# A hybrid-layer kernel: block-sum transfers issued one at a time at a fixed interval, unit loads written where a raw tile is freed, and a bank of its own for a unit's last product

## The chip, the cores and the metric

One core of a Trainium2 chip runs the whole program. The metric is the device time of one execution in microseconds (us), compared by medians of several runs. "Before" is the kernel that is changed, "after" the changed one.

## The reference

The layer has 512 tokens of width 1024. A normalised input is multiplied by one wide matrix `w_in`. Its columns feed a gated delta rule (branch a, 8 heads), a retention (branch b, 4 heads) and two gates. Both branches are projected, gated, mixed by `w_out` and added to the input; then a squared-ReLU MLP with 4096 hidden columns follows.

```python
xn = rmsnorm(x, n_mix_pre)
proj = xn @ w_in
qa, ka, va, za, beta_logit, a_dt, qb, kb, vb, gb, gate_a, gate_b = _split_cols(proj, IN_SIZES)
...
oa = chunk_gated_delta_rule(qa, ka, va, beta, g)
oa = rmsnorm(oa, norm_a) * jax.nn.silu(za.reshape(b, s, A_HEADS, A_DV))
ya = oa.reshape(b, s, A_V) @ w_br_a
...
ob = chunk_retention(qb, kb, vb)
ob = rmsnorm(ob, norm_b.reshape(B_HEADS, B_DV)) * jax.nn.silu(gb.reshape(b, s, B_HEADS, B_DV))
yb = ob.reshape(b, s, B_V) @ w_br_b
mix = (jax.nn.sigmoid(gate_a) * ya + jax.nn.sigmoid(gate_b) * yb) @ w_out
x = x + rmsnorm(mix, n_mix_post)
hn = rmsnorm(x, n_mlp_pre)
ff = jnp.square(jax.nn.relu(hn @ w_up)) @ w_down
return x + rmsnorm(ff, n_mlp_post)
```

## The kernel before

**Products.** Every fp32 operand is split into a high and a low part of type float32r, and a product is three matmuls (high by high, high by low, low by high). Weights come in tiles of 128 x 1024 floats (512 KB): SyncE (SP) issues the load into a tile `raw`, ScalarE (ACT) makes `whi` of it (line 145), VectorE (DVE) makes `wlo` (line 146), TensorE (PE) uses both. The raw tiles are a ring of two, from the first gate unit on of four (a second pool alternates); `whi` and `wlo` are rings of three. So a load waits for the split two or four loads earlier.

**Seven products for eight.** Ten large products are done by a scheme with seven block products instead of eight. It needs sums of weight blocks, and these are made in device memory by transfers alone: a copy job (line 166, on SP's queue) writes a block to a tile `sums`, and an add job (line 132, on GpSimd's queue, POOL, a transfer that accumulates) adds a second block to it. Each job moves 512 KB. There are 56 copies and 56 adds, for the late gates of branch a (`z`, 8 and 8), gate a (4 and 4), four value-and-gate units (4 and 4 each), gate b (4 and 4) and three groups of `w_down` (8 and 8 each), in that order. Adds of a set come after all copies of that set; from then on adds and copies of the next sets alternate.

**When a job is issued.** `pace` (line 112) is called behind each weight load. It compares `spent`, a planner's clock of PE's time, with `queued`, the time until which it takes the transfers to be busy, and issues jobs behind this load as long as `queued` is less than 6 us ahead. Each load counts 2.0 us, a copy 2.0 and an add 3.4, and nothing is issued until the clock is at 150. Several jobs can go behind one load. `issue_after` fixes where they stand in the order; a job runs when its engine's queue reaches it and its data are there.

**The order of each engine's work.** In the first phase (branch a, up to about 480 us of the trace) PE's order is planned by the same clock: steps of the delta rule (the chain) stand between pieces of large products (the fillers). Elsewhere, and on the other engines, a scheduler places instructions by priority; each engine then runs its list strictly in order.

**The units.** After the first phase, gate a, four value-and-gate units and gate b run through `seven` (line 243). In a unit the products are called 11, s3, s2, 12, 22, s1 and s4, each with two weight tiles (`ks` 0 and 1). Between them `plus` (line 249) adds one raw tile to another on DVE, so that a block sum that is not in memory is made from tiles that are there. s1 and s4 share a bank: `out(1, 1, c, u3, ...)` reads s1 from it, s4 is then accumulated on top, and `out(0, 1, c, p1, ...)` reads both. The six units are followed by the mix: PE multiplies `og` by the kept weights of `w_br_b`, transposes gated rows (`tr<-cmat,tb`), and multiplies by `w_out` (row tiles 2 and 3 together, then 0, then 1).

**Around the mix.** `acc` is read last in the gating (lines 1645 to 1649); then POOL loads the rows of x into it for the residual (line 1727), and the rows `post` and `wmlp` of the norm weights (line 1665). Line 1718 (`fw`) multiplies the product of `w_out` by `post`, which also frees the PSUM bank that the next row tile's product writes.

Of the kernel before, what the change touches and what calls it, by code (L numbers as in the profile page):

```python
# [15 lines left out]
ALU = mybir.AluOpType  # L16
# [9 lines left out]
OFF_BA = 6144  # L26
OFF_QB, OFF_KB, OFF_VB, OFF_GB = 6160, 7184, 8208, 10256
OFF_GA, OFF_GBR = 12304, 13328
JOBS_FROM, LOAD_US, COPY_US, ADD_US, BACKLOG = 150.0, 2.0, 2.0, 3.4, 6.0
SMALL_US, CONV_US, TOK_US, PK_US, INV_US, DB_US = 10.5, 6.5, 2.5, 2.0, 46, 1.2  # L30
VT_US, KS_US, PX_US, PC_US, GATE_US, FEAT_US, INV_PRIO, CONV_PRIO, SMALL_PRIO, KEY_PRIO, DECAY_US, AHEAD, TR_US, REC_PRIO, OUT_PRIO, SUM_PRIO = 2.5, 2.4, 3.5, 2.4, 11.0, 1.0, 0, 600, 800, 600, 20.0, 700, 2.2, 900, 900, 300
DFF = 4096
# [30 lines left out]
def hybrid_block_kernel(ctx: ExitStack, tc: tile.TileContext, a: dict, out: bass.AP):  # L63
    nc = tc.nc
# [9 lines left out]
    trickle, later_adds = [], []  # L74
    added, spent, queued, clocks = [False], [None], [JOBS_FROM], []
# [4 lines left out]
    psm = ctx.enter_context(tc.tile_pool(name="psm", bufs=4, space=PSUM))  # L80
# [15 lines left out]
    def weights(src, k0, nk, c0, ncols, keep=None, paced=True):  # L96

        n = nk * ncols
        i = next(loads)
        pool, tag = raw_pools[i % len(raw_pools)]  # L100
        raw = pool.tile([P, 1024], F32, tag=tag, name="raw", bufs=2)
        load = nc.sync.dma_start(
            raw[:, :n].rearrange("p (k c) -> p k c", k=nk),
            src[k0 * P : (k0 + nk) * P, c0 : c0 + ncols].rearrange("(k p) c -> p k c", p=P),
        )
        pace(load)
        with ExitStack() as behind:
            for mark in marks if i < 9 else ():
                behind.enter_context(tc.issue_after(mark.ins))
            return split_weights(raw, n, nk, keep, ahead[0] if i >= 6 else 0)  # L110

    def pace(load):

        if clocks:
            spent[0] = clocks[0].now
        if spent[0] is None:
            return
        queued[0] = max(queued[0], spent[0]) + LOAD_US
        with tc.issue_after(load.ins):
            while (trickle or later_adds) and queued[0] < spent[0] + BACKLOG:  # L120
                ready = bool(later_adds) and not any(job[0] is later_adds[0][2] for job in trickle)
                if ready and (added[0] or not trickle):
                    add_block()
                    queued[0] += ADD_US
                elif trickle:
                    copy_block()
                    queued[0] += COPY_US
                added[0] = not added[0]

    def add_block():  # L130
        dst, src, _ = later_adds.pop(0)
        tc.keep_in_program_order(nc.gpsimd.dma_start(dst, src, accum_op=ALU.add))  # L132

    def copy_block():
        sums, part, k = trickle.pop(0)
        sums.copy(part, k)

    def split_weights(raw, n, nk, keep=None, ahead=200):
        if keep is None:
            hi = ring.tile([P, 1024], F32R, tag="whi", name="whi")  # L140
            lo = ring.tile([P, 1024], F32R, tag="wlo", name="wlo")
        else:
            hi, lo = keep
        with tc.high_priority(ahead):
            nc.scalar.copy(hi[:, :n], raw[:, :n])  # L145
            nc.vector.tensor_tensor(lo[:, :n], raw[:, :n], hi[:, :n], ALU.subtract)  # L146
        return (
            hi[:, :n].rearrange("p (k c) -> p k c", k=nk),
            lo[:, :n].rearrange("p (k c) -> p k c", k=nk),
        )  # L150
# [74 lines left out]
    def bank(pool):  # L225
        if pool is psx:
            return [psx.tile([P, T], F32, tag="dl", name="dl", bufs=3) for _ in range(2)]
        return [psm.tile([P, T], F32, tag="mm", name="mm") for _ in range(2)]
# [13 lines left out]

    def seven(src, c1, c2, sums, product, temp, out):

        def times(pss, x, raws, first):
            for ks in range(2):
                product(pss, x, ks, split_weights(raws[ks], 1024, 2), first)

        def plus(dst, raws):
            with tc.high_priority(SUM_PRIO):  # L250
                for d, r in zip(dst, raws):
                    nc.vector.tensor_tensor(d, r, d, ALU.add)

        def raws(load, i):
            return [load(i, ks) for ks in range(2)]

        p1, u3 = [temp("p1") for _ in range(2)], [temp("u3") for _ in range(2)]
        x, y = raws(sums.first_raw, 1), raws(sums.raw, 3)
        a = bank(psx)
        times(a, "11", x, True)  # L260
        with tc.high_priority(400):
            for t in range(2):
                nc.scalar.copy(p1[t], a[t])
        b = bank(psm)
        times(b, "s3", y, True)
        plus(y, x)
        with tc.high_priority(400):
            for t in range(2):
                nc.vector.tensor_tensor(u3[t], p1[t], b[t], ALU.add)
        x = raws(sums.first_raw, 3)  # L270
        c = bank(psm)
        times(c, "s2", y, True)
        with tc.high_priority(400):
            for t in range(2):
                nc.vector.tensor_tensor(p1[t], p1[t], c[t], ALU.add)
                nc.vector.tensor_tensor(u3[t], u3[t], c[t], ALU.add)
        times(a, "12", x, False)
        out(0, 0, a)
        plus(x, y)
        d = bank(psm)  # L280
        times(d, "22", x, True)
        out(1, 0, d, u3, ALU.add)
        c = bank(psm)
        times(c, "s1", raws(sums.raw, 1), True)
        out(1, 1, c, u3, ALU.subtract)
        times(c, "s4", raws(sums.first_raw, 2), False)
        out(0, 1, c, p1, ALU.subtract)

    def token_product(quarters):

# [22 lines left out]
    def feature_major(src, xs, c0, ncols, kts, krow0=0):  # L313

        nf = ncols // P
        pss = [psm.tile([P, xs[0].shape[2]], F32, tag="mm", name="mm") for _ in range(nf)]
        step = 1024 // ncols
        for k0 in range(0, kts, step):
            wh, wl = weights(src, krow0 + k0, step, c0, ncols)
            for f in range(nf):  # L320
                fs = slice(f * P, (f + 1) * P)
                for kk in range(step):
                    kt = k0 + kk
                    mm3(
                        pss[f],
                        (wh[:, kk, fs], wl[:, kk, fs]),
                        (xs[0][:, kt, :], xs[1][:, kt, :]),
                        kt == 0,
                        kt == kts - 1,
                    )  # L330
        return pss
# [116 lines left out]
    with tc.tile_pool(name="xp", bufs=2) as xp:  # L448
# [3 lines left out]
        first = xp.tile([1, 1], F32, name="first", bufs=1)  # L452
# [15 lines left out]
        xts, raws = [], []  # L468
# [41 lines left out]
        def banks(n):  # L510
            return [psx.tile([P, 2, 256], F32, tag="dl", name="tr", bufs=3) for _ in range(n)]
# [32 lines left out]
        pss = banks(3) + [psx.tile([P, 2, 256], F32, tag="tr", name="tr", bufs=1)]  # L544
# [39 lines left out]
        pss = banks(3)  # L584
# [329 lines left out]
    def acc_rows(t, half):  # L914
        return acc_t[:, t, half * 512 : half * 512 + 512]
# [532 lines left out]
    with tc.tile_pool(name="pb", bufs=1) as pb_:  # L1448
# [11 lines left out]
        def values_and_gates(sums, c1, c2, g, out1, out2):  # L1460

            def out(th, ch, ps, u=None, op=None):
                for t in range(2):
                    row = 2 * th + t
                    if ch:
                        nc.vector.tensor_tensor(g[:, row, :], ps[t], u[t], op)
                        out2(row)
                    elif u is None:
                        out1(row, ps[t])
                    else:  # L1470
                        v = tmp("v_s")
                        nc.vector.tensor_tensor(v, ps[t], u[t], op)
                        out1(row, v)

            seven(w_in, c1, c2, sums, token_product(quarters), tmp, out)
# [90 lines left out]
        def gate_unit(sums, off, gated):  # L1566

            def out(th, ch, ps, u=None, op=None):
                for t in range(2):
                    src = ps[t]  # L1570
                    if u is not None:
                        src = tmp("g_s") if th and not ch else u[t]
                        with tc.high_priority(400):
                            nc.vector.tensor_tensor(src, ps[t], u[t], op)  # L1574
                    gated(2 * th + t, ch, src)

            seven(w_in, off, off + 512, sums, token_product(quarters), tmp, out)

        rows = None
        for h in range(4):  # L1580
# [13 lines left out]
            else:  # L1594
                for half, pss in branch_partial(w_br[1], og, 4 * (h - 1)):
                    for t in range(4):
                        dst = acc_rows(t, half)
# [32 lines left out]
        for pair in (1, 0):  # L1630
            pss = [[psm.tile([P, T], F32, tag="mm", name="mm") for _ in range(2)] for _ in range(2)]
            for i in range(2):
                t = 2 * pair + i
# [26 lines left out]
    with tc.tile_pool(name="pm", bufs=1) as pm:  # L1660
# [215 lines left out]
        for grp in range(4):  # L1876
            sq = Squares(grp)
            for half in range(2):
                for th in (None,) if grp or half else (1, 0):
                    tt = slice(0, T) if th is None else slice(256 * th, 256 * th + 256)  # L1880
                    pss = feature_major(w_up, [h[:, :, tt] for h in hn], grp * 1024 + half * 512, 512, 8)
# [57 lines left out]
```

## Time and profile before

| | |
|---|---|
| three runs | 1342.81, 1347.69 (median), 1348.85 us |
| profiled execution | 1347.26 us, of which the profile's span is 1345.5 us |
| PE, DVE, ACT, POOL busy | 98%, 69%, 47%, 6% of the span |
| clock granted to PE | full speed in all slices |
| transfers | 210.57 MB, a mean of 157 GB/s |
| copy jobs | 56 on SP's queue, median time to landing 7.4 us (`w_in`) and 12.5 us (`w_down`) |
| add jobs | 56 on POOL's queue, median 8.1 us (`w_in`), 14.3 us (`w_down`), 8.3 us (from `sums`) |
| weight loads | median 4.8 us (`w_in`), 4.0 us (from `sums`) |

PE is the engine to look at, so the useful views are its waits and the stretches in which its busy time falls short of the stretch's length. An idle engine elsewhere matters only where PE waits for it. Lines of the kind "start, duration, engine, line, operation" are from the timeline; in brackets stands the idle time before, and what ended it. `raw<-in_w_in_dram SPq` names a transfer by what it writes and reads and by the queue that issues it; its last number is the time from issue to landing.

### The profile page before, as it was taken

What the parts mean: (1) busy time and instruction counts of PE and PEld (TensorE: products, weight loads), DVE (VectorE), ACT (ScalarE), POOL (GpSimd) and SP (SyncE); (2) the same over time, 40 slices, a digit from 0 to 9 for tenths busy, and PEclk for the clock granted to TensorE, in tenths of its full rate; (3) what the DMA queues carried; (4) which work ended last, traced back from release to release, by engine and by line L of the source; (5) the groups of instructions that cost most, each with busy time, mean ns of one, the idle gap of its engine ahead of it and who ended that gap; (6) DMA issues with size and microseconds to landing.
All of it is one profiled execution on the core that took longest, in us unless ns stands there. A gap on an engine that the chain in (4) does not pass through costs nothing.

```text
span 1345.5 us, 17468 instructions
## 1 busy us (share of the span) xinstructions
PE 1324.8 (98%) x6615; PEld 1096.7 (82%) x6615; DVE 930.4 (69%) x1563; ACT 638.3 (47%) x1126; POOL 78.3 (6%) x83
## 2 busy tenths in 40 slices
PE   9999999999999999999999999999999999999997
PEld 7888888878788878888888888877889888888886
DVE  6889867486557567877577776878684745828535
ACT  5783436545534433543443343445255746346441
POOL 2100002010111100001001010000000000000000
PEclk9999999999999999999999999999999999999999
DMA  6322258777889764799398394445614443635421
GB/s 193 128 79 80 69 141 177 160 175 189 226 193 212 176 170 120 238 248 240 91 266 207 103 252 104 129 135 172 221 63 148 163 143 110 188 98 177 133 79 63
DMA packets 105701, 210.57 MB, mean 157 GB/s; under 512 B 6598, under 2 KB 30320, under 8 KB 105104
## 3 DMA queue, kind: packets, MB, share of 16 engines
q1 hardware_dynamic: 88592, 167.27, 39.7%
q0 software_dynamic: 14704, 35.30, 15.6%
q10 hardware_dynamic: 2320, 6.89, 1.4%
q8 instruction: 52, 0.85, 0.3%
q14 instruction: 33, 0.27, 0.1%
HBM read 205.21 MB, written 62.93 MB: 199 GB/s over the span
## 4 chain that ended last, share of the span: by engine, by line
PE 83%; DVE 7%; ACT 4%; DMA 4%; issue 1%; DVEq 0%; ACTq 0%
PE mm L654 15%; PE mm L303 14%; PE mm L93 11%; PE mm L92 11%; PE mm L94 11%; PE dl L303 9%; PE dl L654 5%; DVE wlo L146 2%; DMA raw<-in_w_in_dram 2%; DMA raw<-sums 2%; PE dl L94 1%; PE dl L92 1%; PE dl L93 1%; PE tr L383 1%; PE tr L663 1%
## 5 line engine op out<-in xcount | busy, mean ns | idle before, releaser
L145 ACT CAST whi<-raw 128x1024 fp32r<-128x1024 f32 x259 | 272.1, 1052 | 415.3 <-PE mm L93 104.1
L146 DVE TENSOR_TENSOR wlo<-raw,whi 128x1024 fp32r<-128x1024 f32 x259 | 316.0, 1223 | 216.3 <-ACT whi L145 215.1
L654 PE MATMUL mm<-actT,whi 128*128 128x512 f32 x448 | 144.3, 403 | 0.0
L303 PE MATMUL mm<-whi,xsum 128*128 128x512 f32 x384 | 122.0, 391 | 0.4 <-DVE u L1574 0.4
L94 PE MATMUL mm<-hn,wlo 128*128 128x512 f32 (+1 forms) x288 | 105.4, 366 | 0.0
L93 PE MATMUL mm<-hn,whi 128*128 128x512 f32 (+1 forms) x288 | 105.3, 366 | 0.0
L92 PE MATMUL mm<-hn,whi 128*128 128x512 f32 (+1 forms) x288 | 105.3, 366 | 0.0
L654 PEld LDWEIGHTS mm<-actT,whi 128*128 128x128 f32 x448 | 80.5, 188 | 14.9
L654 PE MATMUL mm<-actT,wlo 128*128 128x512 f32 x224 | 87.7, 392 | 0.0
L303 PEld LDWEIGHTS mm<-whi,xsum 128*128 128x128 f32 x384 | 72.0, 188 | 17.0 <-issue 2.2
L303 PE MATMUL mm<-wlo,xsum 128*128 128x512 f32 x192 | 75.1, 391 | 0.4 <-DVE wlo L146 0.4
L654 PE MATMUL mm<-whi,og 128*128 128x512 f32 x192 | 62.4, 397 | 0.0
L654 PE MATMUL mm<-whi,actT 128*128 128x512 f32 x176 | 61.3, 410 | 1.0 <-DVE qf L892 1.0
L94 PEld LDWEIGHTS mm<-hn,wlo 128*128 128x128 f32 x288 | 54.3, 189 | 8.8
L93 PEld LDWEIGHTS mm<-hn,whi 128*128 128x128 f32 x288 | 54.3, 189 | 8.7
L92 PEld LDWEIGHTS mm<-hn,whi 128*128 128x128 f32 x288 | 54.3, 189 | 8.7
L303 PE MATMUL dl<-whi,ffq 128*128 128x512 f32 x192 | 61.1, 389 | 0.0
L303 PE MATMUL dl<-whi,actT 128*128 128x512 f32 x192 | 61.1, 389 | 0.0
L1771 DVE TENSOR_TENSOR ffq<-r,ffq 128x512 fp32r<-128x512 f32 (+2 forms) x51 | 33.8, 678 | 29.1 <-ACT ffq L1771 29.0
L92 PE MATMUL mm<-actT,whi 128*128 128x512 f32 x128 | 51.5, 403 | 0.0
L132 POOL DMA_DIRECT2D sums<-in_w_in_dram x28 | 32.6, 1167 | 321.3 <-DMA sums<-in_w_in_dram 321.0
L94 PE MATMUL mm<-actT,wlo 128*128 128x512 f32 x128 | 50.8, 397 | 0.0
(393 smaller groups left out, 2881.8 us busy)
## 6 DMA issues: line engine op xcount, KB each, us to landing
raw<-in_w_in_dram SPq DMA_DIRECT2D x95, 512.0 KB, 4.8
raw<-sums SPq DMA_DIRECT2D x56, 512.0 KB, 4.0
raw<-in_w_up_dram SPq DMA_DIRECT2D x36, 512.0 KB, 3.9
sums<-in_w_in_dram SPq DMA_DIRECT2D x32, 512.0 KB, 7.4
sums<-in_w_in_dram POOLq DMA_DIRECT2D x28, 512.0 KB, 8.1
raw<-in_w_down_dram SPq DMA_DIRECT2D x26, 512.0 KB, 3.8
sums<-in_w_down_dram SPq DMA_DIRECT2D x24, 512.0 KB, 12.5
sums<-sums POOLq DMA_DIRECT2D x16, 512.0 KB, 8.3
```

The lines of the kernel that those rows point to most:

```text
L92: nc.tensor.matmul(ps, lh, rh, start=first, stop=False)
L93: nc.tensor.matmul(ps, lh, rl, start=False, stop=False)
L94: nc.tensor.matmul(ps, ll, rh, start=False, stop=last)
L132: tc.keep_in_program_order(nc.gpsimd.dma_start(dst, src, accum_op=ALU.add))
L145: nc.scalar.copy(hi[:, :n], raw[:, :n])
L146: nc.vector.tensor_tensor(lo[:, :n], raw[:, :n], hi[:, :n], ALU.subtract)
L303: m = nc.tensor.matmul(pss[t], lhs[i // 2], rhs[i % 2], start=first and k + i == 0, stop=k + i == 5, skip_group_check=not first,)
L383: nc.tensor.transpose(ps, src, ident)
L654: m = tc.keep_in_program_order(nc.tensor.matmul(*args, **kwargs))
L663: tc.keep_in_program_order(nc.tensor.transpose(ps, src, ident if by is None else by))
L1771: return nc.scalar.copy(dst[0], r), nc.vector.tensor_tensor(dst[1], r, dst[0], ALU.subtract)
```

## The change

Three edits. Jobs go one at a time: `pace` issues at most one job behind a load, and only when the planner's clock has reached `queued`, which then moves on by 8 us; it starts at 65 instead of 150. In `seven` the load of a following raw tile is written directly behind the product that uses the tile it takes the place of, one tile at a time, together with the `plus` for that tile. And s4 gets a bank of its own: the new DVE subtraction `p1 = c - p1` reads s1, and the last `out` adds s4's bank to it.

```diff
-JOBS_FROM, LOAD_US, COPY_US, ADD_US, BACKLOG = 150.0, 2.0, 2.0, 3.4, 6.0
+JOBS_FROM, JOB_US = 65.0, 8.0
...
-        queued[0] = max(queued[0], spent[0]) + LOAD_US
+        if spent[0] < queued[0] or not (trickle or later_adds):
+            return
+        queued[0] += JOB_US
         with tc.issue_after(load.ins):
-            while (trickle or later_adds) and queued[0] < spent[0] + BACKLOG:
-                ready = bool(later_adds) and not any(job[0] is later_adds[0][2] for job in trickle)
-                if ready and (added[0] or not trickle):
-                    add_block()
-                    queued[0] += ADD_US
-                elif trickle:
-                    copy_block()
-                    queued[0] += COPY_US
-                added[0] = not added[0]
+            ready = bool(later_adds) and not any(job[0] is later_adds[0][2] for job in trickle)
+            if ready and (added[0] or not trickle):
+                add_block()
+                added[0] = False
+            else:
+                copy_block()
+                added[0] = True
...
-        def times(pss, x, raws, first):
+        def times(pss, x, raws, first, then=lambda ks: None):
+            out = []
             for ks in range(2):
                 product(pss, x, ks, split_weights(raws[ks], 1024, 2), first)
-
-        def plus(dst, raws):
+                out.append(then(ks))
+            return out
+
+        def plus(dst, other):
             with tc.high_priority(SUM_PRIO):
-                for d, r in zip(dst, raws):
-                    nc.vector.tensor_tensor(d, r, d, ALU.add)
+                nc.vector.tensor_tensor(dst, other, dst, ALU.add)
+
+        def added(dst, other, load, i):
+
+            def then(ks):
+                plus(dst[ks], other[ks])
+                return load(i, ks)
+
+            return then
...
-        times(b, "s3", y, True)
-        plus(y, x)
+        x = times(b, "s3", y, True, added(y, x, sums.first_raw, 3))
...
-        x = raws(sums.first_raw, 3)
...
-        times(a, "12", x, False)
+        y = times(a, "12", x, False, added(x, y, sums.raw, 1))
         out(0, 0, a)
-        plus(x, y)
         d = bank(psm)
-        times(d, "22", x, True)
+        x = times(d, "22", x, True, lambda ks: sums.first_raw(2, ks))
         out(1, 0, d, u3, ALU.add)
         c = bank(psm)
-        times(c, "s1", raws(sums.raw, 1), True)
+        times(c, "s1", y, True)
         out(1, 1, c, u3, ALU.subtract)
-        times(c, "s4", raws(sums.first_raw, 2), False)
-        out(0, 1, c, p1, ALU.subtract)
+        with tc.high_priority(400):
+            for t in range(2):
+                nc.vector.tensor_tensor(p1[t], c[t], p1[t], ALU.subtract)
+        d = bank(psm)
+        times(d, "s4", x, True)
+        out(0, 1, d, p1, ALU.add)
```

The order moves at three places. The first is **SP's queue** around the first loads from `sums` (the late gates `z`); `L166` is a copy job, `L102` and `L194` are weight loads. Before:

```order
L166 DMA sums<-in_w_in_dram 128x2x512
L102 DMA raw<-in_w_in_dram 128x4x256
L166 DMA sums<-in_w_in_dram 128x2x512
L102 DMA raw<-in_w_in_dram 128x4x256
L166 DMA sums<-in_w_in_dram 128x2x512
L102 DMA raw<-in_w_in_dram 128x4x256
L102 DMA raw<-in_w_in_dram 128x2x512
L166 DMA sums<-in_w_in_dram 128x2x512
L102 DMA raw<-in_w_in_dram 128x2x512
L194 DMA raw<-sums 128x1024
L166 DMA sums<-in_w_in_dram 128x2x512
L194 DMA raw<-sums 128x1024
```

The same stretch now:

```order
L166 DMA sums<-in_w_in_dram 128x2x512
L102 DMA raw<-in_w_in_dram 128x4x256 x2
L166 DMA sums<-in_w_in_dram 128x2x512
L102 DMA raw<-in_w_in_dram 128x4x256
L102 DMA raw<-in_w_in_dram 128x2x512
L166 DMA sums<-in_w_in_dram 128x2x512
L102 DMA raw<-in_w_in_dram 128x2x512
L194 DMA raw<-sums 128x1024
L166 DMA sums<-in_w_in_dram 128x2x512
L194 DMA raw<-sums 128x1024
```

The loads stand in the same order; the copy between the first two of them is gone. Over the whole queue, counting all of SP's other transfers, the first copy stood behind the 32nd and now stands behind the 19th, and the last one stood behind the 140th and now stands behind the 164th.

The second place is the **end of POOL's queue**, around the mix (`acc` takes the rows of x; `post` and `wmlp` are norm weights; `sums` are adds). Before:

```order
L132 DMA sums<-in_w_down_dram 128x2x512 x2
L1727 DMA acc<-in_x_dram 128x1024 x4
L1665 DMA post<-in_norm_mix_post_dram 128x1024
L1665 DMA wmlp<-in_norm_mlp_pre_dram 128x1024
L1665 DMA post<-in_norm_mlp_post_dram 128x1024
```

Now:

```order
L132 DMA sums<-in_w_down_dram 128x2x512 x2
L1738 DMA acc<-in_x_dram 128x1024 x2
L132 DMA sums<-in_w_down_dram 128x2x512
L1738 DMA acc<-in_x_dram 128x1024
L132 DMA sums<-sums 128x1024 x2
L132 DMA sums<-in_w_down_dram 128x2x512
L1738 DMA acc<-in_x_dram 128x1024
L1676 DMA post<-in_norm_mix_post_dram 128x1024
L1676 DMA wmlp<-in_norm_mlp_pre_dram 128x1024
L132 DMA sums<-sums 128x1024
L1676 DMA post<-in_norm_mlp_post_dram 128x1024
L132 DMA sums<-sums 128x1024
```

The eight adds of the last set (its last two, at the very end of the queue, are not shown) now stand among and behind these loads, four of them ahead of `post`. Each of the two `sums<-sums` adds ahead of `post` reads what the add before it wrote, and waits for its landing.

The third place is **DVE's list** in a value-and-gate unit, at the change from s1 to s4 (`gs` is the gate's tile, `wlo` the low half of a weight tile). Before:

```order
L1466 TENSOR_TENSOR gs<-mm,u_5011 128x512
L1466 TENSOR_TENSOR gs<-mm,u_5012 128x512
L146 TENSOR_TENSOR wlo<-raw,whi 128x1024 x2
L1466 TENSOR_TENSOR gs<-mm,p_5009 128x512
L1466 TENSOR_TENSOR gs<-mm,p_5010 128x512
```

Now:

```order
L1477 TENSOR_TENSOR gs<-mm,u_5014 128x512
L295 TENSOR_TENSOR p_5012<-mm,p_5012 128x512
L1477 TENSOR_TENSOR gs<-mm,u_5015 128x512
L295 TENSOR_TENSOR p_5013<-mm,p_5013 128x512
L146 TENSOR_TENSOR wlo<-raw,whi 128x1024 x2
L1477 TENSOR_TENSOR gs<-mm,p_5012 128x512
L1477 TENSOR_TENSOR gs<-mm,p_5013 128x512
```

The two new subtractions stand ahead of two splits, the first of which makes `wlo` of s4's second weight tile. On PE the list of the first phase is the same; in each of these units two matmuls of the retention's output that stood in front of s4 now stand behind it, and in the mix the first transposes of gated rows stand two products later.

## The prediction

> **What bounds the kernel now.** I read first the page's busy times and its chain of work, then a table of stretches, then PE's waits.
>
> ```profile
> span 1345.5 us, 17468 instructions
> PE 1324.8 (98%) x6615; PEld 1096.7 (82%) x6615; DVE 930.4 (69%) x1563; ACT 638.3 (47%) x1126; POOL 78.3 (6%) x83
> PE 83%; DVE 7%; ACT 4%; DMA 4%; issue 1%; DVEq 0%; ACTq 0%
> ```
>
> ```profile
> 41.00:475.00 434.00, 426.47 (x2375) 351.48 (x2374) 307.58 (x643) 221.74 (x502) 40.72 (x38) 1.00 0.63 153
> 475.00:870.00 395.00, 394.29 (x1791) 325.62 (x1790) 293.49 (x411) 164.61 (x225) 26.43 (x26) 1.00 0.67 182
> 870.00:960.00 90.00, 88.35 (x407) 71.44 (x406) 76.59 (x108) 42.94 (x60) 1.70 (x3) 1.00 0.49 152
> 960.00:1013.00 53.00, 52.85 (x284) 45.19 (x283) 36.02 (x89) 26.64 (x58) 2.11 (x4) 1.00 0.44 148
> 1013.00:1345.00 332.00, 324.74 (x1487) 270.67 (x1487) 191.22 (x251) 159.35 (x239) 0.00 (x0) 1.00 0.41 130
> ```
>
> PE is busy for 98% of the span, and no edit removes a matmul. In the second fence each row is a stretch, its length, the busy time of PE, PEld, DVE, ACT and POOL, the granted clock (1.00) and the share of the transfer engines. PE's idle time is 434.00 - 426.47 = 7.5 us in the first phase, 0.7 in the units and 1.8 up to 1013. So the change can win 10 us at the very most. It can lose more: a transfer that comes late adds its whole lateness. PE's waits say which gaps are large:
>
> ```profile
> PE tr L663 <- DVE og L1364: 2.7, 1, 2.7
> PE dl L654 <- ACT vt L1314: 2.6, 1, 2.6
> PE tr L383 <- DVE tb L1649: 0.7, 1, 0.7
> PE mm L303 <- DVE u L1574: 0.4, 1, 0.4
> ```
>
> Two waits of 2.7 and 2.6 us hold 5.3 of the first phase's 7.5; the others there are below 1.1 each.
>
> **The jobs in the first phase.** DVE and ACT are named as releasers, but the chains of waits behind these two gaps (one for 284 to 303, one for 344 to 357) lead to loads:
>
> ```profile
> 286.18 9.64 DMA raw<-in_w_in_dram
> ```
>
> ```profile
> 346.05 6.73 DMA raw<-in_w_in_dram
> ```
>
> ACT's list is strict, and its split of the raw tile stands in it ahead of the work that the delta rule waits for (`vt` L895 and L889, L1314). Late is the load. What runs beside these loads in 262 to 352:
>
> ```profile
> raw<-in_w_in_dram SPq DMA_DIRECT2D x10, 512.0 KB, 5.8
> sums<-in_w_in_dram SPq DMA_DIRECT2D x8, 512.0 KB, 6.8
> sums<-in_w_in_dram POOLq DMA_DIRECT2D x8, 512.0 KB, 7.6
> ```
>
> The load from 286.18 took 9.64 us against a median of 5.8. Two adds stood beside it:
>
> ```profile
> 282.32 1.14 POOL L132 DMA_DIRECT2D sums<-in_w_in_dram  x1 [9.36 <-DMA sums<-in_w_in_dram]
> 284.98 1.14 POOL L132 DMA_DIRECT2D sums<-in_w_in_dram  x1 [1.52 <-DMA sums<-in_w_in_dram]
> ```
>
> At one job per 8 us this stretch of 90 us gets about 11 jobs where it had 16, and at each of the two loads there stands about one add fewer. How much shorter the loads become, no row shows, since there is none beside a copy alone. From below: the load keeps its time, because a copy and an add are still beside it, gain 0. From above: it falls to the median, 3.8 us less at the first and 0.9 at the second, and since smaller neighbours ride along, both gaps may close: -5.6 with the 0.3 us gaps beside them. Between ends this far apart I take half, **-2.8 us**, which is about the first gap alone: its load is 3.8 us over the median, more than the 2.7 us gap, while the second is 0.9 over, less than its 2.6.
>
> The jobs that go earlier, from 78 to 180 us of the trace, I cost at nothing. In 60 to 150 ACT's splits wait for PE alone, and no row of the waits there names a load:
>
> ```profile
> ACT whi L145 <- PE mm L654: 14.6, 6, 4.4
> ```
>
> That wait is 2.4 us a split: a load may come that much later before PE sees it. If this cover is gone, each load pays what is over.
>
> The Trainium skill, "DMA: Bandwidth & Descriptors", section "Queues, rings and completion order", says that a transfer engine goes round between the queue rows that have work, a packet from each. By it SP's transfers and POOL's are two takers, one add fewer in POOL's ring leaves a load's share as it was while any add is there, and the sum here would be 0 instead of -2.8. No run so far shows one or the other.
>
> **The units.** The raw loads that are written earlier in the program keep their places in SP's list, so I cost that edit at nothing: the ring of raw tiles sets when they start, and PE's idle time in 475 to 870 is 0.7 us for all units. The bank of its own is different. Twelve DVE subtractions are new, two in each unit, and the two of them stand ahead of the split that makes s4's second `wlo`. In the first of the value units, DVE:
>
> ```profile
> 591.97 1.28 DVE L1466 TENSOR_TENSOR gs<-mm,u 128x512 f32<-128x512 f32 x2
> 593.55 1.23 DVE L146 TENSOR_TENSOR wlo<-raw,whi 128x1024 fp32r<-128x1024 f32 x1 [0.30 <-ACT whi L145]
> ```
>
> and PE, with the retention's two products, s4's first and s4's first use of that `wlo`:
>
> ```profile
> 592.22 0.39 PE L92 MATMUL dl<-vr,s 128*128 128x512 f32 x1
> 592.80 0.47 PE L303 MATMUL mm<-whi,xsum 128*128 128x512 f32 x1
> 595.86 0.39 PE L303 MATMUL mm<-wlo,xsum 128*128 128x512 f32 x1
> ```
>
> Now s4 may start at 592.22, as the retention's two products stand behind it, and each matmul takes 0.23 us from start to start, so the `wlo` is wanted at 592.22 + 13 x 0.227 = 595.17. DVE does four operations of 0.64 (1.28 / 2) from 591.97, until 594.53, then the split of 1.23: 595.76. That is 0.6 late; the gap of 0.13 ahead of s4 goes (592.80 against 592.22 + 2 x 0.227). Net 0.46 in each of the four value units, 1.8 in all. The wait of 0.4 of gate a's unit (`u` L1574) goes, with one more tenth: -0.5. Sum **+1.3 us**. Below: the split starts on time and only the gaps go, -1.1. Above: in all six units the full two subtractions are on the path, 12 x 0.64 / 2, about +4.
>
> **Ahead of the mix** the transposes stand two products later (2 x 0.23 x 3 matmuls), which covers the 0.7 wait for `tb` L1649: **-0.7**, or 0 if DVE is late by more.
>
> **The end of POOL's queue.** The jobs that went early before now run until here, and `post` stands behind them. The rows of before:
>
> ```profile
> 947.94 0.56 POOL L1727 DMA_DIRECT2D acc<-in_x_dram  x1 [5.86 <-DVE tb L1648]
> ...
> 962.37 0.53 POOL L1665 DMA_DIRECT2D post<-in_norm_mix_post_dram  x1 [1.22 <-PE tr L383]
> 962.89 0.53 POOL L1665 DMA_DIRECT2D wmlp<-in_norm_mlp_pre_dram  x1
> ```
>
> ```profile
> post<-in_norm_mix_post_dram POOLq DMA_DIRECT2D x1, 512.0 KB, 8.2
> wmlp<-in_norm_mlp_pre_dram POOLq DMA_DIRECT2D x1, 512.0 KB, 9.6
> ```
>
> `post` landed at 962.37 + 8.2 = 970.57 and was first read here, on DVE, which frees the bank for PE's next product (second fence):
>
> ```profile
> 977.10 0.69 DVE L1718 TENSOR_TENSOR fw<-mm,post 128x512 f32<-128x512 f32 x1 [6.77 <-ACT junk L1707]
> ```
>
> ```profile
> 978.22 0.39 PE L92 MATMUL mm<-whi,actT 128*128 128x512 f32 x1
> ```
>
> That was 6.5 us early. Ahead of it now stand adds, of which two wait for the landing of the one before. What such adds took in 570 to 810, the fastest of them (issued at 570.91), and a row of POOL's list:
>
> ```profile
> sums<-sums POOLq DMA_DIRECT2D x12, 512.0 KB, 8.0
> ```
>
> ```profile
> sums<-sums POOLq DMA_DIRECT2D x1, 512.0 KB, 5.4
> ```
>
> ```profile
> 604.63 0.85 POOL L132 DMA_DIRECT2D sums<-sums  x1 [11.46 <-DMA sums<-in_w_down_dram]
> 614.74 0.81 POOL L132 DMA_DIRECT2D sums<-sums  x1 [9.25 <-DMA sums<-sums]
> 615.26 3.81 POOL L132 DMA_DIRECT2D sums<-in_w_down_dram  x3
> 636.44 0.85 POOL L132 DMA_DIRECT2D sums<-sums  x1 [17.37 <-DMA sums<-in_w_down_dram]
> ```
>
> The last fence holds a price for adds that lie in the queue together: four issued from 614.74 on were through at 636.44, 21.7 us or 5.4 each. So: the first add follows the row of 947.94, at 948.5. With 8.0 and 0.3 for the issue the second goes at 956.8, the third at 965.1, with a fourth (`sums<-in_w_down_dram`) right behind. These two are through at 965.1 + 8.0 + 5.4 = 978.5, the last row of x 2 us later (from `post` to `wmlp`, 970.57 to 972.49, is 1.9), `post` another 2: 982.5. With `fw`'s 0.69 the bank is free at 983.2, PE wanted it at 978.22: **+5.0 us**. Below: 0, if an add takes up to 6.2 (948.5 + 3 x 6.2 + 0.6 + 9.4 = 977.1). Above, with the 10.1 us from 604.63 to 614.74: third add at 969.3, `post` at 988.8, +11.3.
>
> What is queued behind the waiting adds is the last row of x, `post` and `wmlp`; the row of x is read behind `fw`, and `wmlp` later still. The last adds, behind the second `post`, fall into 1005 to 1030, where the loads are:
>
> ```profile
> raw<-in_w_up_dram SPq DMA_DIRECT2D x5, 512.0 KB, 3.8
> ```
>
> Three adds of 5.4 to 8.0 there may lengthen a load as in the first phase (9.64 - 5.8 = 3.8 more at the worst); I take **+0.5**, between 0 and 3.
>
> **The sum**: -2.8 + 1.3 - 0.7 + 5.0 + 0.5 = +3.3 against the profiled execution's 1347.26 (span 1345.5 and 1.8 around it): 1350.6, and with the 0.4 by which the median of the three runs lies above it **1351.0 us**.
>
> **The rivals.** *Slow adds.* The two dependent adds ahead of `post` cost 10.1 each as at 604.63, beside loads of `w_out` and `w_up`. Then PE waits 11.3 instead of 5.0: 1351.0 + 6.3 = 1357.3. From 9.1 us an add the whole is slower by over 0.5%. For it: the row of 604.63, and that these adds go beside loads. Against it: the median of 8.0 and a transfer share of 0.44 in 960 to 1013 against 0.67 in the units. *All jobs in time.* An add takes 5.4, `post` is there at 974.8, and both gaps of the first phase close: -5.6 + 1.3 - 0.7 = -5.0, so 1342.7; with the lower bound of the units 1340.3. For it: the share of 0.44; against it: one row of 5.4 beside eleven with a higher median. The Trainium skill, the same page's section "Anatomy of one DMA — SWDGE (gpsimd) path", has a fit of 2.0 us and bytes / 436e3, an estimate of 3.2 us for 512 KB; by it too `post` would be in time, but the rows' 5.4 to 10.1 speak against it. *No help in the first phase.* The loads at the two gaps still stand beside a copy and an add and take as long as before: 0 instead of -2.8, 1353.8. For it: in the rows of 262 to 352 loads and jobs all take 5.8 to 7.6, and the jobs get only a third fewer.
>
> **How the numbers follow.** A measurement of this kernel tells about 0.5% from no change, 6.7 us: below 1341.0 is faster, above 1354.4 slower. The forecast has a chance of 0.40, slow adds 0.22, no help 0.20, all in time 0.18. Faster: 0.6 of the last and a twentieth of the forecast, 0.13. Slower: 0.9 of slow adds, 0.4 of no help (its bounds reach over 1354.4) and a tenth of the forecast, 0.32. The rest, 0.55, is the same. The forecast's own range is 1346 to 1355 (the first phase and `post` move against each other by 3 to 5). The range to hold 8 in 10 is 1341 to 1358.5: it leaves out the lower half of "all in time" and the slowest adds.
>
> **What would show it.** In the first phase: PE's waits at L663 for `og` L1364 and at L654 for `vt` L1314 gone or shorter, and the loads there below 6 us. In the units: a wait of PE at L303 for `wlo` near 0.6 at each s4. In the mix: `fw` released by `post` in place of `junk` at about 982, and PE's gap of 5 ahead of the second row tile of `w_out`. The forecast is wrong if the time is below 1346 or above 1355: then either `post` is not what PE waits for, or a load that I cost at nothing (78 to 180 us, or `w_out` beside the late adds) is late on PE's path.

## The result, and the profile after

| | before | after |
|---|---|---|
| median of 20 runs | 1345.26 us | 1351.35 us |
| lowest, highest | 1342.81, 1349.82 | 1347.46, 1356.35 |
| span of the profiled execution | 1345.5 | 1349.0 |

The ratio of after to before is 1.0046, with a 95% interval of 1.0034 to 1.0058: the changed kernel is slower by about 6 us. The two profiled executions lie 3.5 us apart, since that of before was 2.0 us above the median of its runs and that of after 0.5 below; sums of terms below are against these 3.5.

The page of the changed kernel, with the rows that were shown of before:

```profile
span 1349.0 us, 17489 instructions
PE 1324.8 (98%) x6615; PEld 1097.6 (81%) x6615; DVE 935.2 (69%) x1575; ACT 638.0 (47%) x1126; POOL 79.8 (6%) x83
PE 78%; DVE 8%; DMA 6%; ACT 5%; issue 2%; POOL 0%; DVEq 0%; ACTq 0%; POOLq 0%
```

Its table of stretches (length; busy PE, PEld, DVE, ACT, POOL; granted clock; share of the transfer engines; GB/s):

```profile
41.00:475.00 434.00, 429.80 (x2397) 354.42 (x2396) 311.39 (x662) 223.39 (x506) 38.54 (x35) 1.00 0.59 146
475.00:870.00 395.00, 393.63 (x1790) 326.05 (x1791) 297.31 (x409) 165.84 (x224) 21.68 (x21) 1.00 0.65 178
960.00:1013.00 53.00, 46.39 (x231) 38.98 (x230) 32.10 (x78) 23.85 (x53) 8.35 (x10) 0.94 0.55 156
```

and PE's waits, the longest ones:

```profile
PE mm L92 <- DVE nh_v L1720: 6.5, 1, 6.5
...
PE dl L93 <- DVE wlo L146: 1.2, 1, 1.2
...
PE dl L665 <- ACT vt L1325: 1.0, 1, 1.0
```

PE's busy time is the same to a tenth (matmuls at a lower clock count in it), so the two spans differ by idle time. The first phase lost its two large waits: PE is busy for 429.80 of 434.00 us, against 426.47 before. Between 960 and 1013 a new wait of 6.5 us stands, and the granted clock of that stretch is 0.94. The wait's name misleads: `nh_v` is the DVE instruction that stood last before PE went on, while the one that PE waited for is `fw`.

Where the time went can be read by the start of the same matmul in both traces:

| matmul near, before | before | after | difference | what lies between |
|---|---|---|---|---|
| end of the first gap | 310.00 | 307.09 | -2.9 | first gap |
| ahead of the second gap | 345.01 | 342.70 | -2.3 | |
| behind the second gap | 375.08 | 369.50 | -5.6 | second gap |
| start of the retention | 490.04 | 484.47 | -5.6 | |
| in the retention | 510.00 | 505.89 | -4.1 | a wait of DVE for `rope` |
| end of the units | 879.89 | 874.57 | -5.3 | units |
| first product of `w_out` | 970.06 | 964.57 | -5.5 | mix |
| behind the first product | 990.02 | 993.58 | +3.6 | the gap and the slow clock |
| last products | 1337.56 | 1341.10 | +3.5 | MLP |

The load of `rope`, in before (first line) and after, with the time from issue to landing last:

```profile
rope<-in_c_rope_dram ACTq DMA_DIRECT2D x1, 512.0 KB, 5.0
rope<-in_c_rope_dram ACTq DMA_DIRECT2D x1, 512.0 KB, 8.5
```

The end of POOL's list in the changed kernel, around `post`:

```profile
942.60 1.24 POOL L132 DMA_DIRECT2D sums<-in_w_down_dram  x1
...
951.59 0.87 POOL L132 DMA_DIRECT2D sums<-sums  x1 [4.44 <-DMA sums<-in_w_down_dram]
960.52 0.82 POOL L132 DMA_DIRECT2D sums<-sums  x1 [8.07 <-DMA sums<-sums]
961.07 1.47 POOL L132 DMA_DIRECT2D sums<-in_w_down_dram  x1
961.78 1.35 POOL L1738 DMA_DIRECT2D acc<-in_x_dram  x1
962.40 1.28 POOL L1676 DMA_DIRECT2D post<-in_norm_mix_post_dram  x1
```

the chain of waits there:

```profile
962.40 16.18 DMA post<-in_norm_mix_post_dram
```

the first use of `post`, `fw` on DVE:

```profile
978.68 0.69 DVE L1729 TENSOR_TENSOR fw<-mm,post 128x512 f32<-128x512 f32 x1 [12.98 <-DMA post<-in_norm_mix_post_dram]
```

and PE's own rows:

```profile
972.50 0.39 PE L94 MATMUL mm<-keep,actT 128*128 128x512 f32 x1
979.42 0.79 PE L92 MATMUL mm<-whi,actT 128*128 128x512 f32 x1 [6.53 <-DVE nh_v L1720]
980.01 0.63 PE L93 MATMUL mm<-wlo,actT 128*128 128x512 f32 x1
980.44 0.63 PE L94 MATMUL mm<-whi,actT 128*128 128x512 f32 x1
```

The adds go one behind the other's landing, 8.99 and 8.93 us apart. `post` is issued at 962.40, only 0.03 us later than in before, but behind an add of 512 KB, a second add and a row of x in the same queue: it takes 16.18 us where it took 8.2. PE stands from 972.73 to 979.42. Then its matmuls start 0.43 us apart where 0.23 is usual: the clock is at one half. The stretch right behind the gap shows it:

```profile
980.00:984.00 4.00, 4.00 (x11) 3.11 (x10) 2.46 (x10) 2.16 (x7) 0.00 (x0) 0.50 0.37 83
```

### The profile page after: what moved, and what is told of

Read it like the earlier page. It is cut to its first block, busy times and chain, and to the rows that moved or that the text cites. A ratio compares the mean times of both kernels' runs of the same rounds, so it can differ in the third digit from the quotient of the medians.

```text
span 1349.0 us, 17489 instructions
## 1 busy us (share of the span) xinstructions
PE 1324.8 (98%) x6615; PEld 1097.6 (81%) x6615; DVE 935.2 (69%) x1575; ACT 638.0 (47%) x1126; POOL 79.8 (6%) x83
## 4 chain that ended last, share of the span: by engine, by line
PE 78%; DVE 8%; DMA 6%; ACT 5%; issue 2%; POOL 0%; DVEq 0%; ACTq 0%; POOLq 0%
PE mm L665 17%; PE mm L314 12%; PE mm L92 10%; PE mm L93 10%; PE mm L94 10%; PE dl L314 9%; PE dl L665 5%; DVE wlo L146 2%; DMA raw<-in_w_in_dram 2%; DMA raw<-sums 1%; DMA post<-in_norm_mix_post_dram 1%; PE tr L674 1%; PE dl L93 1%; ACT whi L145 1%; PE dl L94 1%
```

## The experiments

Ten kernels ran, each with runs of the kernel before on the same chip. All ratios are to those.

| run | what it is | median | before beside it | ratio (95% interval) |
|---|---|---|---|---|
| e1_pace_alone | new pacing alone | 1355.92 | 1344.72 | 1.0085 (1.0065 to 1.0105) |
| e2_units_alone | units and bank alone | 1361.49 | 1344.72 | 1.0127 (1.0108 to 1.0146) |
| e3_tail_held | after, no jobs around the mix | 1340.12 | 1344.72 | 0.9968 (0.9957 to 0.9980) |
| e6_bank_alone | bank alone | 1342.77 | 1344.72 | 0.9992 (0.9980 to 1.0004) |
| e7_pace_bank | pacing and bank | 1351.47 | 1344.50 | 1.0060 (1.0038 to 1.0081) |
| e8_interval_7_5 | after, interval 7.5 | 1346.66 | 1344.50 | 1.0015 (1.0006 to 1.0025) |
| e9_from_69 | after, from 69 | 1354.34 | 1344.50 | 1.0072 (1.0059 to 1.0085) |
| e10_one_job_less | before, one copy taken out | 1354.80 | 1344.50 | 1.0072 (1.0056 to 1.0089) |
| e11_old_then_paced | old rule to 450, then paced and held | 1348.32 | 1346.05 | 1.0023 (1.0009 to 1.0037) |
| e13_hold_old_loads | e3 with the old loads of the units | 1341.85 | 1346.05 | 0.9967 (0.9953 to 0.9981) |

**The wait for `post`: e3.** The changed kernel, with one condition more, so that the last eight adds go behind both rows of norm weights:

```diff
-        if spent[0] < queued[0] or not (trickle or later_adds):
+        if spent[0] < queued[0] or 900.0 < spent[0] < 955.0 or not (trickle or later_adds):
             return
```

> The changed kernel with no job issued while the planner's clock is between 900 and 955: the last eight adds stand behind both `post` rows in POOL's queue, beside the first w_up loads. Theory A: `post` lands near 965 (PE is 5.5 earlier), the gap of 6.5 and the stretch at half clock go, the rest stays: 1351.35 - 9.0 = about 1342, faster than before by about 0.25%. Rival D: eight adds beside w_up loads make a load late for PE by 3 to 10 us in 1005 to 1060: 1345 to 1352. Rival E: another thing than `post` holds the second row tile there (a norm's result, as the wait's name `nh_v` says): about 1351 still.

Measured: 1340.12, 11 us less than the changed kernel and faster than before. The stretch of the mix in its trace:

```profile
960.00:1013.00 53.00, 52.64 (x306) 46.10 (x305) 36.31 (x88) 28.79 (x66) 2.62 (x3) 1.00 0.48 137
```

and the first use of `post`:

```profile
971.01 0.69 DVE L1729 TENSOR_TENSOR fw<-mm,post 128x512 f32<-128x512 f32 x1 [7.74 <-ACT junk L1718]
```

`fw` waits for `junk` again, as in before, PE is busy for 52.64 of 53.00 and the clock is full. So the adds ahead of `post` are the cause of the gap and of the slow clock behind it. The eight adds lie beside `w_up` loads now; these took 6.2 us at the median in 1000 to 1060 (3.8 in before), and yet from 970 to the end of the products the same matmuls of e3 and before keep one distance (-6.1 to -6.0). Rivals D and E fall: no load was late for PE there, and nothing but `post` held the second row tile.

**The parts by themselves: e1 and e2.** e1 is before with the new `pace` (as in the change's diff); e2 is after with the old `pace` and its constants.

> The kernel before with the new pacing alone (one job each 8 us from 65; units as before). Theory A, read from the trace of after: the pacing makes both the gain of 5.6 us in the first phase (PE's waits at L1364 and L1314 gone) and the loss of 9.0 at `post` (6.5 idle and 2.5 at half clock), and the `rope` load makes 1.5 more: 1345.3 - 5.6 + 1.5 + 9.0 = about 1350. Rival B: the gap ahead of the second row tile comes from the units' new order or bank, so that it is missing here: about 1341. Rival C: the two gaps of the first phase closed for another reason than the jobs: they stay, about 1354 to 1356.

Measured: 1355.92, more than expected. That is in the range of rival C, but the first gap is gone from the trace and 1.2 us of the second is left. The first phase gains 4.8 and `post` costs 7.4 in its trace, near what theory A has; the rest is in the units, in waits that after does not have:

```profile
PE mm L303 <- DVE gs L1466: 4.8, 3, 3.0
```

The longest of them, in the chain, on DVE and on PE:

```profile
768.96 11.05 DMA raw<-in_w_in_dram
```

```profile
781.19 1.22 DVE L146 TENSOR_TENSOR wlo<-raw,whi 128x1024 fp32r<-128x1024 f32 x1 [3.39 <-ACT whi L145]
782.33 1.28 DVE L1466 TENSOR_TENSOR gs<-mm,u 128x512 f32<-128x512 f32 x2
```

```profile
783.16 0.47 PE L303 MATMUL mm<-whi,xsum 128*128 128x512 f32 x1 [3.02 <-DVE gs L1466]
```

A tile of s4 takes 11.05 us to land. Its split stands in DVE's list ahead of `gs`, which reads s1, and s4's first matmul may not write into s1's bank before that. After has the same late load, 10.8 us from 765.43, and PE runs through it without a gap: s4 starts in its own bank, and the late tile is wanted only later.

> The change without its pacing: units rewritten and own bank, jobs as before. Theory A: first phase and `post` as before; in the units about -1 (the waits at s4 and of u L1574 gone, the new subtractions hidden): about 1344. Rival B: the loss at `post` stands here: about 1353. The prediction's own term for the units, +1.3, would give 1346.6, its lower bound -1.1 gives 1344.2.

Measured: 1361.49, the reverse of a small gain. Theory A is wrong here. In the units of its trace PE waits for `osq` and `wlo`:

```profile
PE dl L92 <- ACT osq L1567: 9.9, 2, 6.1
PE mm L314 <- DVE wlo L146: 4.1, 5, 1.4
```

Behind the first of these stands, in the chain of waits from 685 on, a load of 12.66 us. The stretch around it has the transfer engines busy throughout, but so has before (0.99 in 680 to 720, with PE busy for all 40.00), so busy engines alone do not make the wait:

```profile
685.61 12.66 DMA raw<-in_w_in_dram
```

```profile
680.00:720.00 40.00, 33.98 (x141) 26.47 (x140) 23.74 (x41) 13.72 (x22) 5.13 (x5) 0.96 1.04 264
```

`pace` is asked where a load is written in the program, and the rewritten units write loads at other points of the planner's clock. The old rule then puts copies and adds behind other loads. The loads' median in 570 to 810 is 7.8 us here, 5.8 in before and in after.

**The bank: e6 and e7.** e6 is before with this edit alone, e7 has the new pacing besides:

```diff
-        times(c, "s4", raws(sums.first_raw, 2), False)
-        out(0, 1, c, p1, ALU.subtract)
+        with tc.high_priority(400):
+            for t in range(2):
+                nc.vector.tensor_tensor(p1[t], c[t], p1[t], ALU.subtract)
+        d = bank(psm)
+        times(d, "s4", raws(sums.first_raw, 2), True)
+        out(0, 1, d, p1, ALU.add)
```

> The kernel before with the own bank for s4 alone (two more subtractions in each unit; loads and jobs as before). Theory A: like the units of after, the gaps of 0.13 ahead of s4 and 0.4 at gate a go and the late wlo costs nothing visible: -1.1, about 1344.2. The prediction's term: +1.3, about 1346.6. Rival F: the gain in the units of after comes from the loads written earlier, not from the bank: 0, 1345.3.

> The kernel before with the new pacing and the own bank for s4, the unit loads written as before. Theory A: the own bank is worth nothing while loads come in time (e6), but with the paced jobs a load of a unit comes late (11.0 us at 768.96 in e1), and then the shared bank holds s4 back until the late tile's split lets DVE read s1 (waits of 4.8 us for gs L1466 in e1). With the bank these 5 go: e1's 1356 - 5 = about 1351, like the changed kernel. Rival G: it is the loads written earlier that save the units: no gain from the bank, about 1356.

e6 can't be told from before (0.9992, interval 0.9980 to 1.0004); +1.3 us would be 1.0010, outside of it. e7 took 1351.47, against e1's 1355.92 and after's 1351.35: the ratios, 1.0085 and 1.0060, have intervals that overlap, so the runs alone do not show a gain. The traces do: with the bank the waits for `gs` of 4.8 us are gone, and between 510 and the end of the units e7 keeps its distance to before (-0.2), where e1 loses 7.5. (The profiled execution of e7 was its slowest, 1359.00, by a wait of 9.0 us at `post` and waits in the first phase.) By the medians the bank is worth 3 to 5 us with late loads. The rewritten loads add nothing to that; e13 says it again.

**Placing and density in the first phase: e10, e9, e8, e11.** e10 is before with one copy taken out ahead of the load of 9.64 us:

```diff
         queued[0] = max(queued[0], spent[0]) + LOAD_US
+        if 259.0 < spent[0] < 262.0:
+            queued[0] += COPY_US
+            added[0] = not added[0]
+            return
```

> The kernel before with one copy left out between two loads just ahead of the one that took 9.64 us, and one add fewer beside it in consequence; all other jobs at their places, each block one place later. Theory A: that load falls to about 6.5 us as in after, the first gap (2.7 in the profile) goes and the second stays: -2.8, about 1342. Rival J: loads share with jobs whatever their number, the load keeps 9 us and the gap stays: 1345.

The load, issued at 286.06 now, took (the only row of its transfers in 286.0 to 286.2, median us to landing last):

```profile
raw<-in_w_in_dram SPq DMA_DIRECT2D x1, 512.0 KB, 4.4
```

and the first gap is gone (the same matmul stands 3.0 us earlier behind it). In after this load takes 6.5. In before adds stood beside it until 294.71, in e10 until 289.07. The packets of the transfers show what the adds do to the load. In these lines q0 is POOL's queue and q1 is SP's; packets, MB and a share of the engines' time follow. Before, in the 4.1 us behind the load's issue (286.2 to 290.3):

```profile
q0 software_dynamic: 299, 0.58, 108.3%
```

e10, in 286.1 to 287.1 (first line) and 287.1 to 288 (the two others):

```profile
q0 software_dynamic: 80, 0.16, 112.6%
...
q0 software_dynamic: 47, 0.07, 55.0%
q1 hardware_dynamic: 54, 0.06, 41.8%
```

So in before the load did not share the engines with the adds: for 4 us it moved not one packet. Its first packet came 4.2 us behind its issue in before, 3.8 in after (one add, issued 1.7 us ahead of it) and 1.1 in e10. That part of theory A holds, and rival J falls. The forecast of 1342 does not hold, by 13 us: a second gap of 3.2 stands in the trace, and three waits of the shared bank (`u` and `gs`, 4.0 together) came up in the units, where each later block now goes one place later. The time of 1354.80 lies above the profiled run's 1350.03, so part of it no trace shows.

e9 and e8 are the changed kernel with one number altered:

```diff
-JOBS_FROM, JOB_US = 65.0, 8.0
+JOBS_FROM, JOB_US = 69.0, 8.0
```

```diff
-JOBS_FROM, JOB_US = 65.0, 8.0
+JOBS_FROM, JOB_US = 65.0, 7.5
```

> The changed kernel with the first job at 69 in place of 65, half an interval later; the same number of jobs, behind other loads. Theory A (density): the first gap stays closed, the second is small; `post` is late as in after or a little later: 1350 to 1354. Rival I (placing): the gaps closed because jobs happened to miss the two loads; then one or both come back: 1353 to 1358.

> The changed kernel with an interval of 7.5 in place of 8.0; all adds but one stand ahead of the rows of x then, and `post` behind no dependent add. Theory A: `post` in time, no gap at the second row tile; first phase between that of after and before: if the gaps hang on how many jobs stand beside a load, one gap may come back in part. 1340 to 1344. Rival H: the loss at `post` has little to do with how many adds stand ahead of it: about 1351.

In e9 the first gap stays closed, and in the place of the second stand two waits for `st` L1315 of 4.4 together; the time of 1354.34 is 3 us above after's, just above theory A's range and within rival I's. The new pacing closes the first gap in every run but one (e7 had 1.0 left); the second is taken up below. In e8 one add stands among the rows of x ahead of `post` in place of four, and `post` is in time; of the second gap small waits of 0.5 to 0.7 are left. So rival H falls. Its median of 1346.66 is above the 1340 to 1344 of theory A and above e3's, while its profiled run of 1343.41 is in the lower part of its runs. Why the others are slower, no trace shows.

e11 is after with the old rule until the clock is at 450, then the new one, held as in e3 (the old rule's loop is left out here, it stands in the change's diff):

```diff
-        if spent[0] < queued[0] or not (trickle or later_adds):
+        if spent[0] < 450.0:
...
+            return
+        if spent[0] < queued[0] or 900.0 < spent[0] < 955.0 or not (trickle or later_adds):
             return
```

> The changed kernel with the old rule for jobs up to a clock of 450, the interval of 8 behind it, and no job from 900 to 955. Theory A: the first phase is as before (its two gaps and their half clock stay, +5.1 against e3 by the traces), units and end as in e3: about 1340.1 + 5.1 = 1345. If the 16.8 us that e2 lost in the units came from the old rule there, nothing of it shows here. Rival K: the gain of the first phase in e3's trace is mostly scatter between executions: 1341 to 1343. Rival L: the units' loss in e2 comes from the rewritten loads whatever the rule: 1355 or more.

Measured: 1348.32, with both gaps back:

```profile
PE dl L679 <- ACT vt L1339: 2.9, 1, 2.9
PE tr L688 <- DVE og L1389: 2.6, 1, 2.6
```

Theory A had 1345. Against e3, which has the new rule from the start, this is 1.0023 to 0.9968, some 7 us. Of the 7.2 us between their two traces, by the starts of the same matmuls, 4.2 arise between 280 and 310, at the first gap and at half clock behind it, and nothing (-0.3) between 310 and 375, at the second; 1.6 are there at 280 already, and 1.7 come behind the first phase. So rival K falls, and the size is about 4 us, all of it at the first gap.

The second gap differs between executions of one order. Up to 490 every engine of e2 and e6 runs before's list, with the old rule. Their first gaps are 2.3 and 2.5 us, but the second has 1.0 and 1.5 where before's trace has 2.6. The two waits in e6:

```profile
PE tr L667 <- DVE og L1368: 2.5, 1, 2.5
PE dl L658 <- ACT vt L1318: 1.5, 1, 1.5
```

Between 310 and 375 e2 and e6 gain 4.2 and 3.7 us on before's trace with no change there at all; after, e1 and e3, with the new rule, gain 2.7, 1.7 and 2.0, and the other runs with it lie between a loss of 0.3 (e9) and a gain of 4.7 (e13). So the runs show that the new rule closes the first gap, and don't show that it does anything for the second.

e11 also has the rewritten units without e2's loss (from 490 to 900 it loses 1.6 us against before, e2 18): the old rule made that loss, together with the rewritten loads.

e13 is e7 with the condition of e3:

> e3 (paced, bank of its own, jobs held around the mix) with the units' loads written as before. Theory A: the rewritten loads are worth nothing where the jobs are paced, so this is e3 again: 1340. Rival M: they help a little as they bring tiles earlier: 1342 to 1345.

Measured: 1341.85, with a ratio of 0.9967 against e3's 0.9968: theory A holds.

## Why the prediction came out

The predicted time was 1351.0, measured were 1351.35. That they agree to 0.4 us is luck: the prediction put +3.3 on 1347.69, the median of three runs of before, while twenty runs have 1345.26, so that by the medians the change costs 6.1. In the two traces, too, the sum came out by terms that miss in both directions:

| term | predicted | measured in the trace |
|---|---|---|
| jobs in the first phase | -2.8 (0 to -5.6) | -5.6: -2.9 at the first gap, -2.7 at the second |
| `rope`, not foreseen | 0 | +1.5 |
| units | +1.3 (-1.1 to +4) | -1.2 |
| ahead of the mix | -0.7 | -0.2 |
| `post` | +5.0 (0 to +11.3) | +9.1 |
| late adds beside `w_up` | +0.5 | 0.0 |
| sum | +3.3 | +3.6 |

Without the second gap, whose 2.7 us the runs do not show to come from the change, the measured terms make +6.3, which is near the 6.1 of the medians.

- **The first phase.** The mechanism (a late load beside adds) is shown by e10, and the size of -2.8, "about the first gap alone", is what that gap gave: -2.9 in after, and 4.2 between e3 and e11. It was half of a bound, so the size was a choice and not a working. The second gap closed in after too, but for 1.0, and before had lost 1.6 us behind it at half clock (against the same matmuls of after); executions of before's order without the change gain as much there.
- **The rule that spoke against it.** From the Trainium skill, "DMA: Bandwidth & Descriptors", section "Queues, rings and completion order", by which transfer engines go round between queue rows, the prediction had worked out a gain of 0. That working was wrong: at this place the load did not share with the adds, it stood behind them, so that one add fewer lets it start earlier (first packet 1.1 us behind its issue in e10, 4.2 in before; 4.4 and 9.64 us to landing). Elsewhere the two queues did move data side by side, 0.29 MB of POOL's and 0.28 of SP's in 484.1 to 488 of after. What decides between the two no run shows, and so the rule itself stays open here.
- **The units** rested on a wrong reading of the order. The two splits behind the new subtractions were said to begin with s4's second tile, here and in the section on the change. They are those of the next product. In after the split at 587.95 (s4's second) stands ahead of the subtractions, which run from 589.68 on, and PE goes through without a gap. What went is the waits at s4, as the lower bound had it (-1.1, measured -1.2). That a shared bank also turns a late tile into a wait was not seen at all.
- **Ahead of the mix** the wait for `tb` L1649 went, but one of 0.7 for `og` (L380) came up, so only 0.2 of the 0.7 was gained.
- **`post`**: the mechanism, the place and the waiting instruction were right. The size was not: two adds took 9.0 each in place of 8.3, and `post` and its use came 18.9 us behind the last dependent add in place of 18.1 (960.52 to 979.42, against 965.1 to 983.2), so that the gap is 6.7 against 5.0; and 2.4 came on top from the half clock behind the gap, of which the prediction had nothing. The rival of slow adds, with 11.3, was nearer to the loss of 9.1, but put it all on the adds.
- **The rivals**: "all jobs in time" did not come (e8 and e3 show what it is worth), "no help in the first phase" is refuted by e10 and e11.
- **A load costed at nothing.** ACT issues the load of `rope` in after 5.6 us earlier than in before (484.03 against 489.62), as PE is early by 5.6, but it took longer: 8.5 us in place of 5.0. DVE waited for it 6.0 us, in before 2.55, and PE lost 1.5. In after an add was under way at its issue (479.26 to 488.14). So it was in seven of the twelve traces, and there this load took 7.3 to 9.3 us; in the five others it took 5.0 to 5.2. The prediction looked for loads that the jobs delay at 78 to 180 us and beside the last adds, not here.
- **The edit costed at nothing**, the unit loads, is worth nothing with the new pacing (e13 against e3, e7 against after). Its cover was the new rule: with the old one it costs some 18 us (e2 against e6).

## What to carry to other kernels

Spreading background transfers evenly takes stalls out where they stood, but a slower rate means a later end: look at what stands behind the last of them in the same queue, above all a transfer that someone waits for. A rule that places work by where the program asks it has every rewriting of the code as an input. A bank shared by two successive products costs next to nothing until a load is late; then it passes a wait on that a second bank would have absorbed. And one trace of each kernel is not enough to size a gap: e2 and e6 have another second gap than before, with the same lists on every engine.

## What was not expected of the hardware

PE's clock falls to one half for a while behind a gap, and this adds to the gap's price. Behind the waits of 6.5 (after), 4.8 (e1), 6.1 and 3.8 (e2), 9.0 (e7) and 6.5 us (e9) matmuls start 0.43 us apart for 3 to 5 us; against the same matmuls of before, 1.8 to 2.6 us were lost each. Shorter gaps do it at times, for 1.3 to 1.8 us: 3.0 us in e1 and 2.6 in e11 (first two lines below), the 2.6 in before (third line), and even 1.4 in e7 (last line). But the 2.7 in before and the 2.9 in e11 were followed by full speed, so the length of the gap alone does not decide it.

```profile
784.00:788.00 4.00, 4.00 (x12) 3.14 (x11) 0.74 (x1) 0.56 (x2) 0.40 (x1) 0.57 0.99 242
304.00:308.00 4.00, 3.42 (x12) 2.91 (x12) 2.68 (x4) 1.21 (x2) 0.00 (x0) 0.57 1.06 188
356.00:359.00 3.00, 3.00 (x9) 2.34 (x8) 2.54 (x4) 1.54 (x5) 0.00 (x0) 0.50 0.40 125
508.00:511.00 3.00, 3.00 (x7) 2.40 (x8) 2.92 (x5) 0.62 (x1) 0.00 (x0) 0.50 0.97 349
```

The third line also corrects the table on the time before: the digit for every slice means 90% or more, so it is not full speed throughout.

The Trainium skill, "TensorE: Matmul & The Clock Gate", section "HAM oscillation — how this bites in real kernels", gives as its rule that PE shouldn't stand idle for more than about 3.4 us, and the same page has a half-rate clock behind that. The traces agree for every gap of 3.8 us and more; the gap of 1.4 in e7 shows that a much shorter one can be enough.

The second point is the load of e10's section: issued while two adds were in flight, it moved nothing for 4.2 us.

The third is the tail of a queue: `post` is a transfer of 512 KB like the others, issued within 0.03 us of its old time, and took twice as long because three transfers stood ahead of it on POOL's queue.
